# Layer norms applied in full with tokens on partitions, in a Mamba-2 and stick-breaking trunk on one core

## Chip, core and metric

The kernel runs on one core of a Trainium2 chip. The metric is the device time of one execution in microseconds (us). Runs of the same kernel differ by some tenths of a per cent: before the change the median of three runs is 1481.68 us (1478.76 to 1482.41).

## What is computed

Input and output are 512 tokens by 1024 channels in float32. The trunk has two layers. The first mixes tokens with a chunked state-space scan (SSD), the second with stick-breaking attention; an MLP with squared ReLU follows each. After each of the four sub-layers a layer norm is applied to the scaled residual plus the sub-layer's output:

```python
def layer_norm(x, g, b):
    mu = jnp.mean(x, axis=-1, keepdims=True)
    var = jnp.mean(jnp.square(x - mu), axis=-1, keepdims=True)
    return (x - mu) * lax.rsqrt(var + LN_EPS) * g + b

for layer in range(2):
    mix = mamba2_mixer(h, ...) if layer == 0 else stick_breaking_attention(h, ...)
    h = layer_norm(ALPHA * h + mix, ln_mix_g[layer], ln_mix_b[layer])
    h = layer_norm(ALPHA * h + squared_relu_mlp(h, ...), ln_mlp_g[layer], ln_mlp_b[layer])
```

So each norm's result has two uses: it is the input of the next sub-layer's matmuls, and it is the residual `h` that the sub-layer after it adds to.

## The kernel before

**Stages.** In order of time: the SSD mixer (to about 470 us), the first MLP (to about 820), attention (to about 1110), the second MLP (to the end). Every float32 matmul is made of three float32r matmuls (`mm3`, lines 159 to 162) on a rounded high part and a low part. So each operand is split: a copy to float32r gives the high part (`hh`, `wh`, `sp..h`, `w..h`), and a subtraction on VectorE (DVE) the low part (`hl`, `wl`, and so on). Weights come in tiles of 512 KB on SyncE's DMA queue in one fixed stream (`emit_w`): a transfer into a raw tile, a ScalarE copy (line 143) and a subtraction (line 145), mostly on DVE.

**Order.** The program is written for a tile framework that works out dependencies and semaphores. At build time it simulates the program and sets each engine's order of instructions from that; on the chip each engine works through its own list in that order. Within attention a hand-written filler spreads the projections of the next heads between the steps of 48 units (`z_stage`, `w_stage`, `pv_stage`).

**Output projections and norms.** `tok_out` computes a sub-layer's output with tokens on partitions. It adds it to the residual `v` (four token tiles of 128x1024) and takes statistics with `bn_stats`. In the last pass it works through the tokens in pairs of tiles (`PAIRS`), and for each pair calls the norm (`Norm.__call__`), and somewhat later its `turn`:

- `__call__` aggregates the statistics on DVE (line 284) and makes the inverse standard deviation with two small GpSimd steps (lines 286 and 287). For the first three norms one DVE `tensor_scalar` for each tile of 1024 columns then subtracts the mean and scales (line 300). The last norm, which has no successor, applies weight and bias too, from rows that are broadcast to all partitions: in two halves of 512 columns, two DVE instructions each (lines 293 and 295).
- `turn` transposes the pair in chunks on TensorE into PSUM (line 319). Channels now lie on partitions, so the norm's weight and bias are one number for each partition, and two ScalarE activations of 128x256 apply them on the way to a tile `hf` (line 322). DVE makes the high part with a cast (line 326) and the low part with a subtraction (line 327).

`v` itself then holds the normalised rows without weight and bias, and needs them before it can serve as the residual. `residual` does this on GpSimd: a multiplication and an addition for each 128x512 piece (lines 334 and 335), 16 instructions for each of the three norms. In the MLPs the 16 are emitted in one go after the first four output tiles (line 371). In attention one pair of them is emitted with every second unit (line 964). The rows for it are loaded on ScalarE's DMA queue by `load_rows` into one of the five large activation buffers.

**Covering work.** When the second pair of tokens is being normalised, TensorE already works on the first pair's columns of the next stage: in an MLP `proj` is called for 256 columns at a time over four output tiles (lines 366 to 368), in attention for the first key, query and value tiles (lines 932 to 936).

Of the kernel before, what the change touches and what calls it, by code (L numbers as in the profile page):

```python
# [11 lines left out]
F32 = mybir.dt.float32  # L12
# [5 lines left out]
P = 128  # L18
# [17 lines left out]
def trunk(ctx: ExitStack, tc: tile.TileContext, io):  # L36
# [46 lines left out]
    lnw = cp.tile([P, 4, 2, KD], F32, name="lnw")  # L83
# [175 lines left out]
    class Norm:  # L259
        def __init__(self, v, idx, name, final=False):  # L260
            self.v, self.idx, self.name, self.final = v, idx, name, final
            self.st = lp.tile([P, NT, 2, 6], F32, tag="st", name=f"{name}_st", bufs=2)
            self.mv = lp.tile([P, NT, 2], F32, tag="mv", name=f"{name}_mv", bufs=2)
            self.rs = lp.tile([P, NT], F32, tag="rs", name=f"{name}_rs", bufs=2)
            self.hl = None
            self.rows = None

            self.tmp = None

        def load_rows(self, pool):  # L270
            if pool is None:
                rows = act_tile(f"{self.name}_r").rearrange("p k t -> p (k t)")
                self.rows = [rows[:, j * D:(j + 1) * D] for j in range(2)]
            else:
                self.rows = [pool.tile([P, D], F32, tag=f"lnr{j}", name=f"{self.name}_r{j}", bufs=1)
                             for j in range(2)]
            for j in range(2):
                nc.scalar.dma_start(self.rows[j], io["lnrow"][self.idx, j].partition_broadcast(P))

        def __call__(self, grp):  # L280
            v, nm = self.v, self.name
            t0, t1 = grp[0], grp[-1] + 1
            for t in grp:
                nc.vector.bn_aggr(self.mv[:, t, :], self.st[:, t, :, :].rearrange("p m s -> p (m s)"))  # L284
            rs = self.rs[:, t0:t1]
            nc.gpsimd.tensor_scalar(rs, self.mv[:, t0:t1, 1], LN_EPS, None, ALU.add)  # L286
            nc.gpsimd.tensor_tensor(rs, rs, mhalf.to_broadcast([P, t1 - t0]), op=ALU.pow)
            if self.final:
                for t in grp:
                    for n in range(2):  # L290
                        c = slice(n * T, (n + 1) * T)
                        vs = v[:, t, c]
                        nc.vector.scalar_tensor_tensor(vs, vs, self.mv[:, t, 0:1], self.rows[0][:, c],
                                                       ALU.subtract, ALU.mult)
                        nc.vector.scalar_tensor_tensor(vs, vs, self.rs[:, t:t + 1], self.rows[1][:, c],
                                                       ALU.mult, ALU.add)
                        nc.sync.dma_start(io["out"][t * P:(t + 1) * P, c], vs)
                return
            for t in grp:
                nc.vector.tensor_scalar(v[:, t, :], v[:, t, :], self.mv[:, t, 0:1], self.rs[:, t:t + 1],  # L300
                                        ALU.subtract, ALU.mult)

        def turn(self, grp):
# [8 lines left out]
            for mm in range(KD // 2):  # L312
                pt = psum("bg", [P, 2, w], f"{nm}_b{mm}{t0}")
                hf = self.tmp[0].tile([P, T], F32, tag=self.tmp[1], name=f"{nm}_f{mm}{t0}", bufs=2)
                hf = hf.rearrange("p (j w) -> p j w", j=2)
# [4 lines left out]
                for j in range(2):  # L320
                    m = 2 * mm + j
                    nc.scalar.activation(hf[:, j, :], pt[:, j, :], AF.Identity,
                                         bias=lnw[:, self.idx, 1, m:m + 1], scale=lnw[:, self.idx, 0, m:m + 1])
                ms = slice(2 * mm, 2 * mm + 2)
                cs = slice(t0 * P, t1 * P)
                nc.vector.tensor_copy(hh[:, ms, cs], hf)  # L326
                nc.vector.tensor_sub(hl[:, ms, cs], hf, f(hh[:, ms, cs]))  # L327

        def residual(self):
            for t in range(NT):  # L330
                for n in range(2):
                    c = slice(n * T, (n + 1) * T)
                    vs = self.v[:, t, c]
                    tc.keep_in_program_order(nc.gpsimd.tensor_mul(vs, vs, self.rows[0][:, c]))
                    nc.gpsimd.tensor_add(vs, vs, self.rows[1][:, c])
                    yield
# [3 lines left out]
    def mlp(layer, ln, nxt):  # L340
        v, (hh, hl) = ln.v, ln.hl
        with tc.tile_pool(name=f"mlp{layer}", bufs=2, reuse_waits="tile") as mp:
            nxt.tmp = (mp, "r")
            ln.load_rows(None)
            for half in range(2):
# [16 lines left out]
                if half == 0:  # L362
# [8 lines left out]
                    for _ in ln.residual():  # L371
                        pass
# [11 lines left out]
                if half == 1 and nxt.final:  # L384
                    nxt.load_rows(mp)
# [5 lines left out]
    def ssm(sp, nxt_ln):  # L391
        nxt_ln.tmp = (sp, "sz")
# [29 lines left out]
        nc.scalar.dma_start(lnw, io["ln"])  # L422
# [290 lines left out]
        for g in range(G):  # L713
# [58 lines left out]
    def attention(ln, nxt):  # L772
# [4 lines left out]
        with tc.tile_pool(name="att", bufs=2, reuse_waits="tile") as at:  # L777
            nxt.tmp = (at, "wl")
            ln.load_rows(None)
# [163 lines left out]
            res = ln.residual()  # L943
            for s in range(len(units) + 3):
# [18 lines left out]
                if s >= 4 and s % 2 == 0:  # L963
                    next(res, None)
# [26 lines left out]
def layout(a):  # L991
# [25 lines left out]
    ln = np.stack([np.stack([a[f"ln_{n}_{s}"][l].reshape(KD, P).T for s in "gb"])  # L1017
                   for l in range(2) for n in ("mix", "mlp")])
    r["ln"] = ln.transpose(2, 0, 1, 3)
# [16 lines left out]
```

## Time and profile before

| | us |
|---|---|
| median of three runs | 1481.68 |
| lowest and highest | 1478.76 and 1482.41 |
| profiled execution | 1479.37 |
| its span, first to last instruction | 1477.6 |
| mean granted TensorE clock in the span | 0.994 |

In the rows, PE is TensorE's matmul work, PEld its weight loads, DVE VectorE, ACT ScalarE, POOL GpSimd and SP SyncE; a letter q behind the name is the engine's instruction queue. A row of a timeline begins with the start in us from the span's start and the duration in us; it names the engine, the line of the kernel, the operation, output<-input, the shapes and the count of instructions merged in it. A bracket at the end tells how long the engine had been idle before, and whose result ended that. Matmuls overlap in the pipeline, so a PE row's duration is longer than the distance to the next one.

### The profile page before, as it was taken

The page shows a single profiled execution, that of the slowest core. Times are in us where ns is not written, and L with a number is a line of the kernel's source. Part 1 is how long each engine was busy: PE and PEld are TensorE (multiplying, and loading weights), DVE is VectorE, ACT ScalarE, POOL GpSimd, SP SyncE. Part 2 cuts the span into 40 slices and gives each one's busy share as a digit, 9 for nine tenths or more (in the row PEclk, how much of TensorE's full clock was granted, in tenths as well). Part 3 has the DMA queues.
Part 4 walks back from the last instruction along what each step waited for, and adds up shares of the span by engine and source line. Part 5 has one row for each costly group of instructions (what it writes and reads, how often), then busy time and mean ns, then how long its engine had stood idle before and what let it go on. Part 6 is the DMA issues. An engine that isn't in the chain of part 4 may idle for free.

```text
span 1477.6 us, 19247 instructions
## 1 busy us (share of the span) xinstructions
PE 1445.0 (98%) x7606; PEld 1239.2 (84%) x7606; DVE 913.7 (62%) x1330; ACT 642.2 (43%) x1032; POOL 293.9 (20%) x291
## 2 busy tenths in 40 slices
PE   9999999999999999999999999999898999999997
PEld 7898897888988888888888997979688888888886
DVE  5799896568876862334423599998849533244334
ACT  5566663356652542123311476767524531133210
POOL 2345453235541610000000123100007000000001
PEclk9999999999999999999999999999999999999999
DMA  5232222322214343333321231111025433233311
GB/s 179 74 113 100 72 61 69 100 72 72 72 43 155 102 128 89 97 100 100 97 90 56 88 99 43 58 57 58 15 60 168 129 100 92 94 100 100 100 43 57
DMA packets 36763, 129.48 MB, mean 88 GB/s; under 512 B 4544, under 2 KB 4800, under 8 KB 36672
## 3 DMA queue, kind: packets, MB, share of 16 engines
q1 hardware_dynamic: 34800, 123.88, 26.6%
q10 hardware_dynamic: 1872, 4.37, 0.9%
q8 instruction: 60, 0.98, 0.3%
q14 instruction: 31, 0.25, 0.1%
HBM read 126.13 MB, written 2.10 MB: 87 GB/s over the span
## 4 chain that ended last, share of the span: by engine, by line
PE 81%; DVE 13%; ACT 2%; issue 2%; DMA 1%; POOL 0%; POOLq 0%; DVEq 0%; SPq 0%; ACTq 0%
PE f L161 16%; PE f L160 16%; PE f L162 16%; PE pz L160 2%; PE pz L162 2%; PE pz L161 2%; PE px L160 2%; PE px L162 2%; PE px L161 2%; DVE wl L145 1%; PE so L162 1%; PE so L160 1%; PE so L161 1%; PE pC L162 1%; PE pC L161 1%
## 5 line engine op out<-in xcount | busy, mean ns | idle before, releaser
L145 DVE TENSOR_TENSOR wl<-wr,wh 128x1024 fp32r<-128x1024 f32 x205 | 260.7, 1273 | 421.6 <-ACT wh L143 420.6
L143 ACT CAST wh<-wr 128x1024 fp32r<-128x1024 f32 x222 | 233.2, 1051 | 528.4 <-PE f L162 251.1
L161 PE MATMUL f<-ln_hl,wh 128*128 128x512 f32 (+1 forms) x576 | 210.0, 367 | 3.4 <-DVE ln_hl L327 3.4
L162 PE MATMUL f<-ln_hh,wl 128*128 128x512 f32 (+1 forms) x576 | 209.6, 366 | 0.0
L160 PE MATMUL f<-ln_hh,wh 128*128 128x512 f32 (+1 forms) x576 | 207.6, 367 | 1.1 <-DVE ln_hh L326 1.1
L286 POOL TENSOR_SCALAR ln_rs<-ln_mv 128x2 f32<-128x2 f32 (+1 forms) x10 | 5.2, 519 | 697.7 <-DVE ln_mv L284 697.7
L161 PEld LDWEIGHTS f<-ln_hl,wh 128*128 128x128 f32 x576 | 108.5, 189 | 21.5 <-DVE ln_hl L327 4.2
L162 PEld LDWEIGHTS f<-ln_hh,wl 128*128 128x128 f32 x576 | 108.6, 189 | 17.6
L160 PEld LDWEIGHTS f<-ln_hh,wh 128*128 128x128 f32 x576 | 107.2, 189 | 19.2 <-DVE ln_hh L326 1.5
L162 PE MATMUL pz<-wh,x_l 128*128 128x256 f32 x256 | 72.7, 284 | 0.0
L161 PE MATMUL pz<-wl,x_h 128*128 128x256 f32 x256 | 72.6, 284 | 0.0
L160 PE MATMUL pz<-wh,x_h 128*128 128x256 f32 x256 | 72.4, 283 | 0.0
L145 POOL TENSOR_TENSOR wl<-wr,wh 128x1024 fp32r<-128x1024 f32 x17 | 43.1, 2536 | 95.1 <-ACT wh L143 78.3
L160 PE MATMUL px<-x_h,wh 128*128 128x512 f32 x128 | 50.8, 397 | 0.0
L162 PE MATMUL px<-x_h,wl 128*128 128x512 f32 x128 | 50.3, 393 | 0.0
L161 PE MATMUL px<-x_l,wh 128*128 128x512 f32 x128 | 50.3, 393 | 0.0
L161 PEld LDWEIGHTS pz<-wl,x_h 128*128 128x128 f32 x256 | 48.8, 190 | 0.8
L160 PEld LDWEIGHTS pz<-wh,x_h 128*128 128x128 f32 x256 | 48.7, 190 | 0.8
L162 PEld LDWEIGHTS pz<-wh,x_l 128*128 128x128 f32 x256 | 48.8, 190 | 0.3
L350 ACT ACTIVATE r<-f 128x512 f32<-128x512 f32 x64 | 37.9, 592 | 20.7 <-DVE hd000l L359 16.3
L856 POOL TENSOR_TENSOR u<-u 128x128 f32<-128x128 f32 x16 | 9.3, 582 | 183.5 <-DVE u L854 183.5
L851 ACT ACTIVATE u<-z 128x384 f32<-128x384 f32 (+1 forms) x48 | 25.0, 524 | 39.4 <-DVE sp200l L860 7.0
(1348 smaller groups left out, 3918.0 us busy)
## 6 DMA issues: line engine op xcount, KB each, us to landing
wr<-w SPq DMA_DIRECT2D x128, 512.0 KB, 3.5
wr<-w_bc SPq DMA_DIRECT2D x16, 512.0 KB, 3.5
wr<-w_x SPq DMA_DIRECT2D x16, 512.0 KB, 3.5
wr<-w_z SPq DMA_DIRECT2D x16, 512.0 KB, 3.5
wr<-w_so SPq DMA_DIRECT2D x16, 512.0 KB, 3.5
wr<-w_qk SPq DMA_DIRECT2D x16, 512.0 KB, 3.6
ln_r<-lnrow ACTq DMA_DIRECT2D x8, 512.0 KB, 5.1
wr<-w_v SPq DMA_DIRECT2D x8, 512.0 KB, 3.6
```

Source lines behind the costliest of these rows:

```text
L143: nc.scalar.copy(hi, raw)
L145: eng.tensor_sub(lo, raw, f(hi))
L160: nc.tensor.matmul(out, a[0], b[0], start=start, stop=False, skip_group_check=skip)
L161: nc.tensor.matmul(out, a[0], b[1], start=False, stop=False, skip_group_check=skip)
L162: nc.tensor.matmul(out, a[1], b[0], start=False, stop=stop, skip_group_check=skip)
L286: nc.gpsimd.tensor_scalar(rs, self.mv[:, t0:t1, 1], LN_EPS, None, ALU.add)
L350: nc.scalar.activation(r, pt, AF.Relu)
L851: nc.scalar.activation(e, z, AF.Abs)
L856: nc.gpsimd.tensor_add(e4[:, n:], e[:, P:2 * P], e[:, 2 * P:])
```

## The change

Weight and bias are applied while tokens lie on partitions, in all four norms. The one `tensor_scalar` becomes two `scalar_tensor_tensor` instructions on DVE: `shift`, (v - mean) * weight row, and `scale`, (v * inverse deviation) + bias row. `turn` then only splits: a ScalarE copy out of PSUM makes the high part, and DVE subtracts it from PSUM for the low part. The residual pass, its rows in an activation buffer, the small table `lnw` and its load are dropped. The rows are loaded ahead of the norm: for the first in 512-column pieces into four buffers of the scan's decay matrices, for the second in whole rows into tiles of their own, for the third in 512-column pieces into the attention's work buffers behind the last unit, and for the last in 512-column pieces.

```diff
-        def load_rows(self, pool):
-            ...
+        def load_rows(self, make, width=D):
+            self.rows = []
+            for c0 in range(0, D, width):
+                seg = [c0, c0 + width]
+                for j in range(2):
+                    r = make(j, c0)
+                    nc.scalar.dma_start(r, io["lnrow"][self.idx, j, c0:c0 + width].partition_broadcast(P))
+                    seg.append(r)
+                self.rows.append(seg)
 ...
+            def shift(t, c0, c1, w):
+                vs = v[:, t, c0:c1]
+                nc.vector.scalar_tensor_tensor(vs, vs, self.mv[:, t, 0:1], w, ALU.subtract, ALU.mult)
+
+            def scale(t, c0, c1, b):
+                vs = v[:, t, c0:c1]
+                nc.vector.scalar_tensor_tensor(vs, vs, self.rs[:, t:t + 1], b, ALU.mult, ALU.add)
+                if self.final:
+                    nc.sync.dma_start(io["out"][t * P:(t + 1) * P, c0:c1], vs)
 ...
             for t in grp:
-                nc.vector.tensor_scalar(v[:, t, :], v[:, t, :], self.mv[:, t, 0:1], self.rs[:, t:t + 1],
-                                        ALU.subtract, ALU.mult)
+                for c0, c1, w, b in self.rows:
+                    shift(t, c0, c1, w)
+            for t in grp:
+                for c0, c1, w, b in self.rows:
+                    scale(t, c0, c1, b)
 ...
-                for j in range(2):
-                    m = 2 * mm + j
-                    nc.scalar.activation(hf[:, j, :], pt[:, j, :], AF.Identity,
-                                         bias=lnw[:, self.idx, 1, m:m + 1], scale=lnw[:, self.idx, 0, m:m + 1])
 ...
-                nc.vector.tensor_copy(hh[:, ms, cs], hf)
-                nc.vector.tensor_sub(hl[:, ms, cs], hf, f(hh[:, ms, cs]))
-
-        def residual(self):
-            ...
+                nc.scalar.copy(hh[:, ms, cs], pt)
+                nc.vector.tensor_sub(hl[:, ms, cs], pt, f(hh[:, ms, cs]))
 ...
     def mlp(layer, ln, nxt):
-            ln.load_rows(None)
 ...
-                    for _ in ln.residual():
-                        pass
 ...
-                if half == 1 and nxt.final:
-                    nxt.load_rows(mp)
+                if half == 1:
+                    nxt.load_rows(lambda j, c0: mp.tile([P, T if nxt.final else D], F32,
+                                                        tag=f"lnr{j}{c0 if nxt.final else 0}",
+                                                        name=f"lnr{layer}{j}{c0}", bufs=1),
+                                  T if nxt.final else D)
 ...
     def ssm(sp, nxt_ln):
-        nc.scalar.dma_start(lnw, io["ln"])
 ...
+                else:
+                    nxt_ln.load_rows(lambda j, c0: sp.tile(S4, F32, tag="dec", name=f"lnr{j}{c0}", bufs=4)
+                                     .rearrange("p a c -> p (a c)"), T)
 ...
     def attention(ln, nxt):
-            ln.load_rows(None)
-            res = ln.residual()
 ...
-                if s >= 4 and s % 2 == 0:
-                    next(res, None)
+            nxt.load_rows(lambda j, c0: at.tile([P, T], F32, tag=("u", "wf")[j], name=f"lnr{j}{c0}", bufs=2), T)
```

## Rows read from the trace of the kernel before

**Rows 1.** The page's first part: busy time, share of the span and instructions of each engine.
```profile
PE 1445.0 (98%) x7606; PEld 1239.2 (84%) x7606; DVE 913.7 (62%) x1330; ACT 642.2 (43%) x1032; POOL 293.9 (20%) x291
```

**Rows 2.** Busy time by stretches of the span. Columns: stretch and its length, busy us and count for PE, PEld, DVE, ACT and POOL, granted TensorE clock, share of DMA engines, GB/s. The first two stretches lie after the first norm, the next two round the third norm, the last is the tail of attention.
```profile
480.00:500.00 20.00, 20.00 (x149) 19.04 (x148) 12.70 (x14) 10.93 (x17) 7.35 (x4) 1.00 0.35 114
500.00:520.00 20.00, 20.00 (x90) 16.57 (x89) 19.93 (x12) 9.90 (x15) 19.53 (x13) 1.00 0.26 80
...
1100.00:1120.00 20.00, 18.84 (x119) 16.55 (x118) 15.24 (x23) 7.98 (x12) 4.94 (x6) 1.00 0.58 180
1120.00:1140.00 20.00, 16.63 (x131) 15.53 (x130) 19.39 (x13) 9.06 (x15) 19.53 (x13) 1.00 0.32 108
...
1040.00:1068.00 28.00, 22.87 (x101) 17.25 (x102) 23.84 (x47) 17.31 (x35) 1.22 (x2) 0.88 0.06 20
```

**Rows 3.** PE's timeline in attention, the rows with an idle time before them.
```profile
917.49 0.50 PE L903 MATMUL o<-w112l,vp 128*128 128x512 f32 x1 [0.67 <-DVE w112l L891]
...
918.90 0.33 PE L883 MATMUL z<-sp200h,none_r 128*128 128x128 f32 x1 [0.80 <-DVE sp200h L859]
...
920.59 0.33 PE L883 MATMUL z<-sp200l,none_r 128*128 128x128 f32 x1 [0.85 <-DVE sp200l L860]
...
978.09 0.44 PE L841 MATMUL z<-q,k 128*128 128x384 f32 x1 [0.88 <-ACT wf L887]
...
979.34 0.46 PE L903 MATMUL o<-w400h,vp 128*128 128x256 f32 x1 [0.57 <-DVE w400h L890]
...
990.68 0.39 PE L841 MATMUL z<-q,k 128*128 128x256 f32 x1 [0.44 <-ACT wf L887]
...
992.43 0.50 PE L903 MATMUL o<-w402h,vp 128*128 128x512 f32 x1 [0.32 <-DVE w402h L890]
```

**Rows 4.** Busy time by stretches, as in rows 2, for the two stretches of attention at a lower granted clock.
```profile
921.47:924.88 3.41, 3.41 (x17) 3.41 (x16) 2.59 (x3) 3.36 (x7) 0.00 (x0) 0.50 0.12 17
979.50:982.91 3.41, 3.41 (x9) 2.76 (x10) 3.28 (x7) 2.02 (x4) 0.00 (x0) 0.50 0.19 78
```

**Rows 5.** DVE's timeline in attention before and during the first gaps of rows 3.
```profile
913.47 0.42 DVE L890 CAST w112h<-wf 128x512 fp32r<-128x512 f32 x1
...
915.76 1.67 DVE L891 TENSOR_TENSOR w112l<-wf,w112h 128x512 fp32r<-128x512 f32 x1
917.36 1.49 DVE L859 CAST sp200h<-u 128x512 fp32r<-128x512 f32 x1
...
919.35 1.19 DVE L860 TENSOR_TENSOR sp200l<-u,sp200h 128x512 fp32r<-128x512 f32 x1
```

**Rows 6.** POOL's timeline at that time: the first and the last of four residual instructions in a row.
```profile
914.17 1.28 POOL L334 TENSOR_TENSOR v<-v,ln_r 128x512 f32<-128x512 f32 x1
...
918.64 1.35 POOL L335 TENSOR_TENSOR v<-v,ln_r 128x512 f32<-128x512 f32 x1
```

**Rows 7.** Groups of DVE instructions by line and shape from 480 to 500 us (after the first norm's second pair). Columns: count, busy us, mean ns of one, idle us before them and what ended it.
```profile
L327 DVE TENSOR_TENSOR ln_hl<-ln_f,ln_hh 128x512 fp32r<-128x512 f32 x4 | 2.8, 692 | 0.1
...
L326 DVE CAST ln_hh<-ln_f 128x512 fp32r<-128x512 f32 x4 | 1.7, 424 | 4.5 <-ACT ln_f L322 4.4
```

**Rows 8.** The same groups from 1120 to 1137 us (after the third norm's second pair).
```profile
L327 DVE TENSOR_TENSOR ln_hl<-ln_f,ln_hh 128x512 fp32r<-128x512 f32 x5 | 8.4, 1678 | 0.1
L326 DVE CAST ln_hh<-ln_f 128x512 fp32r<-128x512 f32 x4 | 5.5, 1367 | 0.5 <-ACT ln_f L322 0.5
```

**Rows 9.** PE's timeline at the start of the second MLP.
```profile
1113.28 0.38 PE L161 MATMUL f<-ln_hl,wh 128*128 128x256 f32 x1 [1.16 <-DVE ln_hl L327]
```

**Rows 10.** DVE's timeline: the first norm of the second pair, a weight subtraction, and one token tile of the last norm.
```profile
476.16 1.53 DVE L300 TENSOR_SCALAR v<-v,ln_mv,ln_rs 128x1024 f32<-128x1024 f32 x2 [0.92 <-POOL ln_rs L287]
...
1103.17 1.22 DVE L145 TENSOR_TENSOR wl<-wr,wh 128x1024 fp32r<-128x1024 f32 x1
...
1456.38 1.41 DVE L295 SCALAR_TENSOR_TENSOR v<-v,ln_rs,ln_r 128x512 f32<-128x512 f32 x2 [0.47 <-POOL ln_rs L287]
```

**Rows 11.** POOL's timeline: the two small steps of a norm, in the second norm and in the last.
```profile
811.99 0.22 POOL L286 TENSOR_SCALAR ln_rs<-ln_mv 128x2 f32<-128x2 f32 x1 [288.74 <-DVE ln_mv L284]
812.29 0.71 POOL L287 TENSOR_TENSOR ln_rs<-ln_rs,mhalf 128x2 f32<-128x2 f32 x1
...
1465.43 0.78 POOL L286 TENSOR_SCALAR ln_rs<-ln_mv 128x1 f32<-128x1 f32 x1 [3.64 <-DVE ln_mv L284]
1466.30 0.92 POOL L287 TENSOR_TENSOR ln_rs<-ln_rs,mhalf 128x1 f32<-128x1 f32 x1
```

**Rows 12.** PE's timeline at the start of the first MLP: two of its first matmuls and the transposes of the second pair.
```profile
470.07 0.28 PE L162 MATMUL f<-ln_hh,wl 128*128 128x256 f32 x1
470.19 0.28 PE L160 MATMUL f<-ln_hh,wh 128*128 128x256 f32 x1
...
479.79 0.60 PE L319 MATMUL ln_b<-ident,v 128*128 128x128 f32 x4
```

**Rows 13.** One line's instructions: a ScalarE copy of a 128x512 tile out of PSUM. Columns: count, shortest, median and longest ns, first and last start.
```profile
L615 ACT COPY cbm<-cb x8: 573/586/597, 65.0 to 417.6; 128x512 f32<-128x512 f32 x8
```

**Rows 14.** The loads of the norms' rows: the issuing instruction, with columns as in rows 13.
```profile
L278 ACTq DMA_DIRECT2D ln_r<-lnrow x8: 334/392/688, 469.7 to 1129.3; - x8
...
DMA to landing us min/median/max: 4.0/5.1/6.2
```

**Rows 15.** PE's timeline at the end of the SSD stage.
```profile
445.76 0.51 PE L160 MATMUL so<-wx,yT4h 128*128 128x512 f32 x1 [1.20 <-DVE v L248]
```

More of the change, by code (lines that the diff above doesn't have):

```diff
@@ L82, in trunk @@
     nw = cp.tile([P, 16], F32, name="nw")
-    lnw = cp.tile([P, 4, 2, KD], F32, name="lnw")
     stream = []
@@ L266, in __init__ @@
             self.rows = None
-            self.tmp = None
-        def load_rows(self, pool):
[L271 to L276, printed above, removed]
-            for j in range(2):
-                nc.scalar.dma_start(self.rows[j], io["lnrow"][self.idx, j].partition_broadcast(P))
+        def load_rows(self, make, width=D):
[7 more added lines that the diff above has]
+                self.rows.append(seg)
         def __call__(self, grp):
@@ L287, in __call__ @@
             nc.gpsimd.tensor_tensor(rs, rs, mhalf.to_broadcast([P, t1 - t0]), op=ALU.pow)
+            def shift(t, c0, c1, w):
[6 more added lines that the diff above has]
+                    nc.sync.dma_start(io["out"][t * P:(t + 1) * P, c0:c1], vs)
             if self.final:
                 for t in grp:
[L290 to L293, printed above, removed]
-                                                       ALU.subtract, ALU.mult)
-                        nc.vector.scalar_tensor_tensor(vs, vs, self.rs[:, t:t + 1], self.rows[1][:, c],
-                                                       ALU.mult, ALU.add)
-                        nc.sync.dma_start(io["out"][t * P:(t + 1) * P, c], vs)
+                    for c0, c1, w, b in self.rows:
+                        shift(t, c0, c1, w)
+                        scale(t, c0, c1, b)
                 return
             for t in grp:
-                nc.vector.tensor_scalar(v[:, t, :], v[:, t, :], self.mv[:, t, 0:1], self.rs[:, t:t + 1],
-                                        ALU.subtract, ALU.mult)
+                for c0, c1, w, b in self.rows:
+                    shift(t, c0, c1, w)
+            for t in grp:
+                for c0, c1, w, b in self.rows:
+                    scale(t, c0, c1, b)
         def turn(self, grp):
@@ L319, in turn @@
                         nc.tensor.transpose(pt[:, j, (t - t0) * P:(t - t0 + 1) * P], v[:, t, m * P:(m + 1) * P], ident)
-                for j in range(2):
-                    m = 2 * mm + j
-                    nc.scalar.activation(hf[:, j, :], pt[:, j, :], AF.Identity,
-                                         bias=lnw[:, self.idx, 1, m:m + 1], scale=lnw[:, self.idx, 0, m:m + 1])
                 ms = slice(2 * mm, 2 * mm + 2)
                 cs = slice(t0 * P, t1 * P)
-                nc.vector.tensor_copy(hh[:, ms, cs], hf)
-                nc.vector.tensor_sub(hl[:, ms, cs], hf, f(hh[:, ms, cs]))
-        def residual(self):
[L330 to L336, printed above, removed]
+                nc.scalar.copy(hh[:, ms, cs], pt)
+                nc.vector.tensor_sub(hl[:, ms, cs], pt, f(hh[:, ms, cs]))
     PAIRS = [(0, 1), (2, 3)]
@@ L391, in ssm @@
     def ssm(sp, nxt_ln):
-        nxt_ln.tmp = (sp, "sz")
         x_h, x_l = act_pair("x_")
@@ L1016, in layout @@
     r["x"] = a["x"][0]
-    ln = np.stack([np.stack([a[f"ln_{n}_{s}"][l].reshape(KD, P).T for s in "gb"])
-                   for l in range(2) for n in ("mix", "mlp")])
-    r["ln"] = ln.transpose(2, 0, 1, 3)
     r["lnrow"] = np.stack([np.stack([a[f"ln_{n}_{s}"][l] for s in "gb"]) for l in range(2) for n in ("mix", "mlp")])
```

4 lines of the change are left out of this document (removed).

## The prediction

> **What bounds the kernel now.** I read the page's busy times first. TensorE (PE) is busy 1445.0 us, 98% of the span [rows 1], and the change alters no matmul and no transpose, so its time can only come from the few places where PE waits or runs at a lower clock. Next I cut the span into stretches [rows 2]. After the first norm PE is busy 20.00 of 20 us, and it stays so in the next stretch, although GpSimd runs the residual pass there and keeps VectorE (DVE) at 19.93. Round the third norm PE is busy 18.84 and then 16.63. So the same pass costs nothing in the first MLP and may cost 3.4 us in the second.
>
> The attention stage is the other place. In its tail PE is busy 22.87 of 28 us [rows 2], but the residual pass is over by then. Earlier, its PE timeline [rows 3] has gaps of 0.67, 0.80 and 0.85 us between 916.8 and 920.6 us (2.32 in sum), each ended by a DVE result, and 2.21 us in four gaps between 977 and 993 us. Each group is followed by 3.41 us in which the granted clock was 0.50 against 1.00, that is 1.2 GHz instead of 2.4 [rows 4]. At half clock PE does 1.7 us of work in those 3.41, so 1.7 us is lost each time.
>
> Then I asked who held DVE up. Just before the first group of gaps a 128x512 two-input subtraction took 1.67 us, a cast 1.49 and another subtraction 1.19 [rows 5], while GpSimd ran four residual instructions back to back [rows 6]. The same cast takes 0.42 a little earlier [rows 5], and the same kind of subtraction 0.69 after the first norm [rows 7]. The excess is 0.98 + 1.07 + 0.50 = 2.55 us: nearly the 2.32 that PE lost. After the third norm the casts average 1.37 and the subtractions 1.68 us [rows 8], against 0.42 and 0.69 for the same lines after the first [rows 7].
>
> That reading has a rule beside it. The Trainium skill (SBUF — State Buffer, section "Who interferes with whom") says that VectorE and GpSimd share one port pair as an exclusive lock, which a cast in a two-port mode, or an instruction with two SBUF inputs against a GpSimd one that reads SBUF, must wait for. The 1.67 against 0.69 us agrees.
>
> **The change, part by part.**
>
> *Residual pass removed in the second MLP.* The five gaps that make the 3.37 us of the 1120 to 1140 stretch [rows 2] end on the slowed casts and subtractions [rows 8]. With no pass beside them they should run as after the first norm, where the same loops left PE no gap [rows 2, 7]: **-3.4**. Bounds 0 (another wait comes next) and -3.4.
>
> *Residual pass removed in attention.* The gaps of 2.32 us go with the excess of 2.55, and with them the half-clock stretch that followed: -2.32 - 1.7 = **-4.0**. Bounds 0 and -4.0. What is late next there is the chain through ScalarE that the later gaps show. The gaps of 977 to 993 [rows 3] come some 57 us later, and two of the four end on a ScalarE exponential rather than on DVE. They can be lag carried over from the slowed part, or DVE's own load. I take half of 2.21 + 1.7: **-2.0**, with bounds 0 and -3.9.
>
> *Norm in two passes.* Before, two tokens' rows were normalised by two one-source instructions, 1.53 us together, after GpSimd's two steps. Now each token tile of 1024 columns takes a shift and a scale, both with two tensor inputs. The last norm has them already: two of 512 columns take 1.41 us [rows 10]. So a pair of tiles costs 8 x 0.70 = 5.6 us of DVE against 1.53 (with 1024 columns in one instruction somewhat less). The shift doesn't need GpSimd's result, so GpSimd's 0.22 and 0.71 us [rows 11] pass beside it: the chain from statistics to the last scale grows from about 1.0 + 1.5 to 5.6, by 3.1 us. Against this stand the four casts of the first pair, now gone from DVE: 4 x 0.42 = 1.7 us [rows 7]. So the second pair's norm ends some 1.4 us later.
>
> What covers this at the first norm: by 470.1 PE is at the first half of the tokens, with 96 matmuls 0.12 us apart, 11.5 us in all [rows 12], and the transposes of the second pair stand at 479.79, while the norm before ended at 476.16 + 1.53 = 477.7 [rows 10, 12]. That is 2.1 us of slack against 1.4. The second norm is built alike. I take **0** for both; if the cover is gone (one weight subtraction of 1.2 us more in front [rows 10]) up to 1.5 us each, so 0 to +3.
>
> A row that speaks against this part: in the last norm GpSimd's two steps took 0.78 and 0.92 us beside the shifts, against 0.22 and 0.71 alone [rows 11]. Even so the 1.7 us pass beside 2.8 us of shifts, and the sum is unchanged. By the rule of that section of the Trainium skill each step may wait for one whole shift, so the 1024-column shifts of the second norm would give 2 x 1.4 + 0.9 = 3.7 us, +0.9 on the chain there.
>
> *After the transposes.* Each chunk of 128x512 had two ScalarE instructions, a DVE cast and a DVE subtraction. Now ScalarE copies once (0.59 us for that shape out of PSUM [rows 13]) and DVE subtracts once, about 0.69. This is shorter by the cast, 0.42 us for each chunk; where PE has no gap it gives nothing: 0. But a PSUM buffer is now held until DVE has read it. That matters at the third norm alone, where the projection's second column half sits in the same four buffers. There PE already waited 1.16 us for the first subtraction [rows 9]. Two opposite effects, the cast gone and the buffer late: **+0.5**, with bounds -1.2 (gap gone) and +2.7 (plus one half-clock loss and a us of its own).
>
> *Rows and the small load.* Three norms now load their two rows early on ScalarE's queue, in the third behind the last attention unit. An issue took 0.39 us in the middle [rows 14], so four cost 1.6 us of that queue. At the end of the SSD stage PE waits anyway (1.20 us at 445.76 [rows 15]) in a chain of weight transfer, copy and subtraction; if the rows' 1 MB stands before a weight tile, a row transfer of 512 KB takes 5 us to land [rows 14]. I take **+0.5**, with bounds 0 and +3. The loads that go (the same rows, later, and the small table) hid under full PE stretches: 0.
>
> Sum: -3.4 - 4.0 - 2.0 + 0.5 + 0.5 = **-8.4 us**. The profiled execution took 1479.37 us, so it would take 1471.0; the median of the three runs is 1481.68, 2.3 above it, and the forecast in those terms is 1473.3 us.
>
> **Rivals.**
>
> *The attention stalls are not GpSimd's.* PE also lost time at 977 to 993 [rows 3], and DVE is nearly full there by its own load, 3.28 of 3.41 us [rows 4]; the lost 2.3 us may come back a few units later. Against it: the excess equals the gaps. Then only the second MLP gains: -3.4 + 1.0 = -2.4, 1479.3 us.
>
> *Full return.* The relieved DVE also clears the later gaps: -3.4 - 1.2 - 4.0 - 3.9 = -12.5, 1469.2 us; clearing some of the 5.1 us that PE lacks in the tail of attention [rows 2] could add 3. For it: that same DVE load. Against it: nothing in the rows ties the stall at 978 us to a GpSimd instruction.
>
> *Slower: PE runs dry at the norms.* The longer DVE chain of the second pair, with weight subtractions queued between, ends after the 11.5 us of covering matmuls are spent. It decides once the chain is later by some 3 to 4 us instead of 1.4. A dry spell of 2 us is what cost a half-clock stretch in attention [rows 3, 4], so each of three norms would lose 2.0 + 1.7, 11 us; with attention's gain undone as well, -3.4 + 11 = +7.6, 1489.3 us. Against it: PE's order fills from 96 independent matmuls.
>
> **How the numbers follow.** Forecast 0.50, full return 0.15, stalls not GpSimd's 0.24, PE dry 0.11. About 0.3% (4.4 us) can be told from no change. The first two lie beyond it: faster 0.65; the third within: 0.24; the last: 0.11. The range reaches from the full return with part of the tail, 1466, over the third case to 1484, with the positive bounds of the norm and row terms; it leaves out most of the dry case.
>
> **What would show it.** Right: no GpSimd instruction over 1 us after 460 us but weight subtractions; casts near 0.42 and subtractions near 0.69 in attention and at the start of the second MLP; PE 20 of 20 us after the third norm; one half-clock stretch fewer in attention. Wrong: PE gaps ended by a shift, a scale or a transpose at any norm; the same gaps in attention with casts at 0.42; a longer PE wait at the end of the SSD stage ended by a transfer.

## The result, and the profile after

| | before | after |
|---|---|---|
| median of 4 runs each, us (lowest to highest) | 1481.95 (1478.76 to 1482.41) | 1466.99 (1466.41 to 1467.21) |
| ratio of times, 95% interval | | 0.9907 (0.9893 to 0.9921) |
| profiled execution, us (span) | 1479.37 (1477.6) | 1466.94 (1464.9) |

The change saves 12.4 us between the two profiled executions and 15.0 between the medians. That is faster, by 0.9% and well beyond the 0.3% that can be told from no change; the forecast was 1473.3 us, within 1466 to 1484. The direction held, and the gain is larger than the forecast 8.4: half as large again between the profiled executions, 1.8 times by the medians.

The page's first part of the changed kernel answers to [rows 1]:

```profile
PE 1439.3 (98%) x7606; PEld 1237.5 (84%) x7606; DVE 880.4 (60%) x1334; ACT 632.2 (43%) x1008; POOL 222.9 (15%) x243
```

GpSimd lost 71 us of work, VectorE 33 and ScalarE 10. The number of matmuls is the same. So what counts is where TensorE waited or ran slowly. Next come stretches of the changed kernel with the columns of [rows 2] and [rows 4]. The first three lie after the first and third norm, the next four cut the span from the second norm to the start of the second MLP into stages, and the last two are the parts of attention at the lower clock.

```profile
480.00:500.00 20.00, 20.00 (x148) 18.93 (x147) 13.92 (x18) 12.54 (x18) 2.44 (x1) 1.00 0.55 183
500.00:520.00 20.00, 20.00 (x90) 16.56 (x89) 9.12 (x12) 8.72 (x12) 0.00 (x0) 1.00 0.37 110
1114.00:1134.00 20.00, 20.00 (x152) 19.21 (x152) 14.37 (x20) 12.54 (x18) 0.00 (x0) 1.00 0.48 154
...
820.00:850.00 30.00, 30.00 (x240) 29.17 (x239) 20.85 (x30) 11.51 (x19) 4.75 (x9) 1.00 0.26 83
850.00:1000.00 150.00, 147.96 (x888) 132.77 (x887) 130.22 (x237) 107.10 (x200) 6.78 (x11) 1.00 0.20 65
1000.00:1096.00 96.00, 90.73 (x455) 76.49 (x454) 70.25 (x130) 47.81 (x87) 4.62 (x7) 0.95 0.16 50
1096.00:1150.00 54.00, 53.76 (x343) 48.55 (x342) 38.47 (x54) 24.29 (x34) 2.49 (x3) 1.00 0.50 160
...
1040.87:1044.28 3.41, 3.41 (x14) 2.92 (x15) 2.38 (x6) 2.25 (x6) 0.00 (x0) 0.50 0.00 0
1051.11:1057.94 6.83, 6.71 (x20) 5.25 (x20) 6.42 (x14) 3.13 (x6) 0.00 (x0) 0.50 0.11 40
```

PE's idle time is a stretch's length less its busy time. From 850 to 1000 us it is 2.04 (4.76 in the same stretch before), from 1096 to 1150 it is 0.24 (4.54 before), and after the first norm 0.00, as it was. Of the half-clock stretches the two of [rows 4] have gone. In the tail of attention the clock is low for 3.41 + 6.83 us, against a single 6.83 (from 1058 us) before.

PE's timeline after, at the places of [rows 15] and [rows 3]; these are its only rows with 0.3 us or more of idle time from 440 to 470 us and from 850 to 1000 us:

```profile
445.70 0.50 PE L159 MATMUL so<-wx,yT4h 128*128 128x512 f32 x1 [1.32 <-DVE v L247]
...
973.20 0.44 PE L829 MATMUL z<-q,k 128*128 128x384 f32 x1 [1.93 <-ACT wf L875]
```

The gaps of 916.8 to 920.6 us are gone, and so is the 1.16 of [rows 9]. The four later gaps of attention have shrunk to one of 1.93, nearly their sum of 2.21.

Where the time went is read best by following the same matmul through both PE timelines (start in us):

| the first matmul that reads | before | after | difference |
|---|---|---|---|
| sp111l with ntri_ge (second head pair) | 903.52 | 903.53 | 0.0 |
| w212l | 949.56 | 943.90 | -5.7 |
| w502l | 1017.45 | 1009.34 | -8.1 |
| sp710l with ntri_ge (last pair) | 1059.83 | 1053.02 | -6.8 |
| ln_hh and wh, second MLP | 1111.21 | 1103.61 | -7.6 |
| (end of the span) | 1477.6 | 1464.9 | -12.7 |

Nothing was gained or lost in the first 903 us. Attention gives 7.6 us, three quarters of it between 903 and 950, and the second MLP gives 5.1. Four transposes of the third norm, 0.4 us of work, stand ahead of the last mark before and behind it after; counted alike, attention gives 7.2 and the second MLP 5.5.

### The profile page after: what moved, and what is told of

It is laid out like the page before. It is cut to its first block, busy times and chain, and to the rows that moved or that the text cites. A ratio compares the mean times of both kernels' runs of the same rounds, so it can differ in the third digit from the quotient of the medians.

```text
span 1464.9 us, 19160 instructions
## 1 busy us (share of the span) xinstructions
PE 1439.3 (98%) x7606; PEld 1237.5 (84%) x7606; DVE 880.4 (60%) x1334; ACT 632.2 (43%) x1008; POOL 222.9 (15%) x243
## 4 chain that ended last, share of the span: by engine, by line
PE 88%; DVE 7%; ACT 2%; DMA 1%; issue 1%; POOL 0%; POOLq 0%; DVEq 0%; SPq 0%; ACTq 0%
PE f L160 16%; PE f L159 16%; PE f L161 16%; PE pz L159 2%; PE pz L161 2%; PE pz L160 2%; PE px L159 2%; PE px L161 2%; PE px L160 2%; PE z L873 1%; PE so L161 1%; PE so L159 1%; PE so L160 1%; PE o L891 1%; PE pv L159 1%
## 5 line engine op out<-in xcount | busy, mean ns | idle before, releaser
L144 DVE TENSOR_TENSOR wl<-wr,wh 128x1024 fp32r<-128x1024 f32 x205 | 252.8, 1234 | 443.8 <-ACT wh L142 443.3
L283 POOL TENSOR_SCALAR ln_rs<-ln_mv 128x2 f32<-128x2 f32 (+1 forms) x10 | 8.9, 887 | 745.8 <-DVE ln_mv L281 745.8
L339 ACT ACTIVATE r<-r 128x512 f32<-128x512 f32 x64 | 40.6, 634 | 2.1
```

The source lines that it names most:

```text
L144: eng.tensor_sub(lo, raw, f(hi))
L339: nc.scalar.activation(r, r, AF.Square)
```

## The experiments

Each is compared with runs of the kernel before on its own chip (medians 1479.44 to 1481.29 us). "The pass" is what GpSimd did for the residual. In kernels built from the changed one it is replayed as two multiplications by one for each 128x512 piece of v, in the same places.

**The kernel before without its pass** (norms and transposes as before; the weight and bias rows and GpSimd's two instructions per piece are out, so the residual lacks them).

```diff
-            ln.load_rows(None)
...
-                    for _ in ln.residual():
-                        pass
...
-            ln.load_rows(None)
...
-            res = ln.residual()
...
-                if s >= 4 and s % 2 == 0:
-                    next(res, None)
```

> The kernel before with the residual pass and the loads of its rows taken out (the residual then lacks the norms' weight and bias; the inputs of the matmuls keep them). Pass theory (GpSimd's pass holds VectorE up in attention and at the start of the second MLP): 1467 to 1471 us, most of the measured gain of 15, with the 1.16 us wait at the third norm left. Split theory (the gain is the shorter way after the transposes): no change, 1480 to 1482. Order theory (the gain comes from another order drawn up at build time): anywhere, with no fewer slowed casts to go with it.

Measured 1469.74 us, ratio 0.9938 (0.9926 to 0.995): dropping the pass alone gives 9.8 us against before's 1479.58, where the changed kernel's repeat, further down, gives 12.6. The start of the second MLP, by stretches:

```profile
1096.00:1150.00 54.00, 52.83 (x339) 47.73 (x338) 35.73 (x54) 26.25 (x40) 2.35 (x4) 1.00 0.43 147
```

The one PE row with over 0.3 us of idle time at the third norm:

```profile
1112.78 0.38 PE L161 MATMUL f<-ln_hl,wh 128*128 128x256 f32 x1 [1.17 <-DVE ln_hl L327]
```

The idle time at the start of the second MLP falls from 4.54 to 1.17 us, by the 3.37 that the prediction put on the pass. What is left is the gap of [rows 9], unmoved. So the pass didn't cause that gap, and the change removes it by its other part. In time the pass cost more than that idle time: from the first matmul of the second MLP (1110.70) to the end of the span (1472.3) this run takes 361.6 us, and before took 366.4. In attention it takes 40.6 us from the sp111l to the w212l of the table above (905.94 to 946.52), against 46.0 before and 40.4 after. Its profiled execution is the slowest of the five (1474.29): it is already 2.6 us late at the first matmul of the first MLP (472.35 against 469.72), so stretches can be compared and starts can't.

**The changed kernel with the pass back in attention alone.**

```diff
+    ones4 = one.unsqueeze(1).to_broadcast([P, 4, P])
...
+    def passes(v, pool):
+        for t in range(NT):
+            for n in range(2):
+                vs = v[:, t, n * T:(n + 1) * T].rearrange("p (a c) -> p a c", a=4)
+                tc.keep_in_program_order(nc.gpsimd.tensor_mul(vs, vs, ones4))
+                nc.gpsimd.tensor_mul(vs, vs, ones4)
+                yield
...
+            res = passes(v, at)
...
+                if s >= 4 and s % 2 == 0:
+                    next(res, None)
```

> The kernel after with 16 GpSimd multiplications of the residual by one (128x512 each, two after every second attention unit, where the pass was). Pass theory: attention is 8 us longer again, 1474 to 1476 us, with gaps on PE ended by casts of 1.4 to 1.5 us. Split theory and order theory: 1466 to 1468.

Measured 1475.18 us, ratio 0.997 (0.9959 to 0.9981): 8.2 us slower than the changed kernel. DVE's timeline at the gaps of [rows 3]:

```profile
916.39 0.93 DVE L857 CAST sp200h<-u 128x512 fp32r<-128x512 f32 x1
917.25 1.43 DVE L857 CAST sp201h<-u 128x384 fp32r<-128x384 f32 x1
918.59 1.75 DVE L858 TENSOR_TENSOR sp200l<-u,sp200h 128x512 fp32r<-128x512 f32 x1
```

POOL's timeline there, the first and the last of four pass instructions in a row, as in [rows 6]:

```profile
914.31 1.29 POOL L334 TENSOR_TENSOR v<-v,ones_r 128x512 f32<-128x512 f32 x1
...
918.54 1.26 POOL L335 TENSOR_TENSOR v<-v,ones_r 128x512 f32<-128x512 f32 x1
```

The PE row with the largest idle time in that place:

```profile
920.40 0.41 PE L881 MATMUL z<-sp200l,none_r 128*128 128x128 f32 x1 [2.29 <-DVE sp200l L858]
```

And the stretch that follows, with the columns of [rows 4]:

```profile
920.50:923.91 3.41, 3.41 (x15) 3.41 (x16) 2.17 (x3) 3.36 (x6) 0.00 (x0) 0.50 0.00 0
```

Four GpSimd instructions in a row, a slowed cast and subtraction, a PE gap of 2.29 (2.32 in three gaps before) and 3.41 us at half clock come back at the same place. The matmuls of the table above then start at 903.77, 949.45, 1017.76 and 1060.34, within 0.5 us of before, and the second MLP's first at 1110.35, 0.9 earlier than before. So at least 6.7 of attention's 7.6 us are the pass's. Each edit also draws up another order of instructions at build time, and that alone could move the time. But the run before this one had the old code without the pass and lost the stalls, and this one has the new code with it and gets them back, with the slowed instructions beside GpSimd's.

**The pass back in the second MLP alone.**

```diff
+                    if layer == 1:
+                        for _ in passes(v, mp):
+                            pass
                     extra[:] = [mp, 2, 2, False, marks[1 + 2 * layer]]
```

(`passes` as in the run before.)

> The kernel after with the same 16 GpSimd multiplications by one at the start of the second MLP, where the pass was. Pass theory as predicted: +4 to +5 us, 1471 to 1472. Pass theory with the port rule taken strictly: VectorE's one instruction for each chunk now reads PSUM and one SBUF tile, which need not wait for GpSimd, so +0 to +1.5 us, 1467 to 1468.5, the scales and weight subtractions alone being slowed. Split theory: no change.

Measured 1469.37 us, ratio 0.9921 (0.991 to 0.9933), 2.4 above the changed kernel by medians: more than the strict rule gave, less than the prediction did. Its DVE groups from 1108 to 1125 us, with columns as in [rows 7]:

```profile
L291 DVE SCALAR_TENSOR_TENSOR v<-v,ln_rs,lnr 128x512 f32<-128x512 f32 x4 | 6.8, 1770 | 0.6 <-POOL ln_rs L284 0.6
L144 DVE TENSOR_TENSOR wl<-wr,wh 128x1024 fp32r<-128x1024 f32 x3 | 6.3, 2137 | 0.4 <-ACT wh L142 0.4
L326 DVE TENSOR_TENSOR ln_hl<-ln_b,ln_hh 128x512 fp32r<-128x512 f32 x4 | 2.6, 681 | 0.1
```

PE's rows with an idle time from 1090 to 1130 us:

```profile
1114.68 0.87 PE L322 MATMUL ln_b<-ident,v 128*128 128x128 f32 x6 [0.52 <-DVE v L291]
1116.36 0.87 PE L322 MATMUL ln_b<-ident,v 128*128 128x128 f32 x6 [0.81 <-DVE v L291]
```

Beside the same GpSimd work the new subtraction, which reads one operand from PSUM, keeps 0.68 us. The scale and the weight subtraction, with two SBUF operands, take 1.77 (0.75 alone) and 2.14 (1.22 alone). The idle time from 1096 to 1150 us is 1.38 against 0.24 us, +1.1. The rest of the 2.4 isn't in this profile, whose execution was the fastest of the five, 1465.15 at a mean clock of 0.997; three others took 1469.4 to 1469.8 at 0.994.

**Before's transposes and split put back** (ScalarE copies out of PSUM in two instructions, DVE casts and subtracts from SBUF), in three forms: with nothing else, with the pass in the second MLP, and with GpSimd there only writing memory.

```diff
-                nc.scalar.copy(hh[:, ms, cs], pt)
-                nc.vector.tensor_sub(hl[:, ms, cs], pt, f(hh[:, ms, cs]))
+                hf = self.tmp[0].tile([P, T], F32, tag=self.tmp[1], name=f"{nm}_f{mm}{t0}", bufs=2)
+                hf = hf.rearrange("p (j w) -> p j w", j=2)
+                for j in range(2):
+                    nc.scalar.activation(hf[:, j, :], pt[:, j, :], AF.Identity)
+                nc.vector.tensor_copy(hh[:, ms, cs], hf)
+                nc.vector.tensor_sub(hl[:, ms, cs], hf, f(hh[:, ms, cs]))
...
```

The third has, in place of the pass's two multiplications:

```diff
+        scr = pool.tile([P, 3 * T], F32, name="scr", bufs=1)
...
-                tc.keep_in_program_order(nc.gpsimd.tensor_mul(vs, vs, ones4))
-                nc.gpsimd.tensor_mul(vs, vs, ones4)
+                tc.keep_in_program_order(nc.gpsimd.memset(scr, 1.0))
+                nc.gpsimd.memset(scr, 2.0)
```

> The kernel after with the old split after the transposes (two ScalarE instructions into an SBUF tile, a cast and a subtraction), and no residual pass. Pass theory: only the wait at the third norm comes back, with one half-clock stretch at most, 1467 to 1471 us. Split theory (the shorter split is worth what the run with old split and pass lost): 1475 to 1482.

> As the run before, but with the old split after the transposes (two ScalarE instructions into an SBUF tile, then a cast and a subtraction that read SBUF). Port rule: casts near 1.4 and subtractions near 1.7 us again, PE gaps of 3 to 5 us after the third norm, 1470 to 1472.5 us. Split theory: the same time, but with casts at 0.42.

> The kernel after with the old split, and at the start of the second MLP 16 GpSimd memsets of 128x1536 (they write and read nothing) where the run with old split and pass had multiplications. Port rule: casts are slowed, subtractions of two SBUF tiles keep 0.69 us; 1470 to 1477 us. If any GpSimd work slows VectorE: as with the pass, 1480 to 1484. If only GpSimd's reads do: as the old split alone.

Measured 1473.61 (ratio 0.9956, 0.9944 to 0.9968), 1482.41 (1.0019, 1.001 to 1.0027) and 1472.68 (0.9954, 0.9942 to 0.9966). The first lies above what the pass theory allowed and below the other, so neither had it: the old split alone costs 6.6 us. Two PE rows of the kernel with the old split alone:

```profile
470.20 0.39 PE L160 MATMUL f<-ln_hl,wh 128*128 128x256 f32 x1 [0.33 <-DVE ln_hl L331]
...
827.21 0.38 PE L161 MATMUL pv<-wh,ln_hl 128*128 128x256 f32 x1 [0.80 <-DVE ln_hl L331]
```

PE now waits for the subtraction at the first norm, where neither kernel of the change does, and for 0.80 us at the second, where before waited 0.16 (at 826.49) and the changed kernel doesn't wait. The second head pair starts 2.8 us late (906.28). Whether this is the old split's doing or that of the long norm beside it is settled further down, with the one-pass norm. Of the rest, a half-clock stretch behind a gap of 1.93 us at 976 us (the repeat of the changed kernel has one too) takes 1.3 us up to w502l, and about 3 us fall between the last head pair and the second MLP, where no run here singles out a cause.

The second adds 8.8 us. The start of its second MLP, by stretches:

```profile
1096.00:1150.00 54.00, 47.39 (x291) 41.82 (x290) 50.39 (x59) 18.62 (x33) 29.27 (x20) 0.94 0.35 120
```

Its DVE groups from 1112 to 1138 us:

```profile
L331 DVE TENSOR_TENSOR ln_hl<-ln_f,ln_hh 128x512 fp32r<-128x512 f32 x7 | 9.7, 1391 | 0.1
L292 DVE SCALAR_TENSOR_TENSOR v<-v,ln_rs,lnr 128x512 f32<-128x512 f32 x4 | 6.8, 1765 | 0.0
L330 DVE CAST ln_hh<-ln_f 128x512 fp32r<-128x512 f32 x6 | 6.8, 1131 | 0.0
```

PE is idle 6.61 us there against 1.05 with the old split alone (+5.6), and a mean clock of 0.94 over 54 us, where it was 1.00, takes some 3.2 more. That adds up to the 8.8 between the medians, but in part by chance: in the two profiled executions the second MLP takes 371.3 us (from 1108.99) against 361.5 (from 1110.73), 9.8 more, since a gap costs more than its idle time. The expectation lacked both the old split's own price and this half clock.

The third runs 16 GpSimd memsets of 1.4 to 1.5 us through the same time. DVE groups from 1116 to 1130 us:

```profile
L330 DVE CAST ln_hh<-ln_f 128x512 fp32r<-128x512 f32 x5 | 5.4, 1087 | 1.1 <-ACT ln_f L329 1.1
L331 DVE TENSOR_TENSOR ln_hl<-ln_f,ln_hh 128x512 fp32r<-128x512 f32 x5 | 3.4, 689 | 0.1
L292 DVE SCALAR_TENSOR_TENSOR v<-v,ln_rs,lnr 128x512 f32<-128x512 f32 x4 | 2.7, 737 | 0.0
```

A GpSimd that only writes slows the casts (1.09 against 0.42 us) and leaves the instructions with two SBUF inputs alone (0.69, 0.74), and PE loses nothing: 0.87 us idle from 1096 to 1150. The Trainium skill (SBUF — State Buffer, section "Who interferes with whom") says just that: an instruction with two SBUF inputs contends with a GpSimd one that reads SBUF, not with one that only writes. These rows agree, and so does the 0.68 of the subtraction out of PSUM beside the reading pass.

**The changed kernel with a one-pass norm** (the first three norms leave out weight and bias).

```diff
-                for c0, c1, w, b in self.rows:
-                    shift(t, c0, c1, w)
...
+                nc.vector.tensor_scalar(v[:, t, :], v[:, t, :], self.mv[:, t, 0:1], self.rs[:, t:t + 1],
+                                        ALU.subtract, ALU.mult)
```

> The kernel after with one tensor_scalar for each tile in the first three norms in place of shift and scale (weight and bias of those norms are left out). If the longer VectorE chain is covered by PE's work on the first pair, as predicted: no change, 1465 to 1468 us. If the chain costs something that PE does not show: 2 us or more faster.

Measured 1469.08 us, ratio 0.9928 (0.9915 to 0.994): no faster than the two-pass norm (1466.99), and rather slower. Its idle time from 820 to 850 us (0.00) and from 1096 to 1150 (0.24) is that of the changed kernel; a gap of 0.92 us at 984.27 is new. Why the shorter norm is 2 us slower stays open beyond that gap.

With it, all four pairings of norm and split have been run. The time from the first matmul of the first MLP to the sp111l of the table above, which holds the first and the second norm, in us:

| | one-pass norm | two-pass norm |
|---|---|---|
| old split | 433.8 (before, 469.72 to 903.52); 433.6 (before without its pass, 472.35 to 905.94) | 436.9 (469.35 to 906.28) |
| short split | 433.8 (469.55 to 903.33) | 433.9 (the changed kernel, 469.66 to 903.53) |

Neither the old split nor the longer norm costs anything there by itself; together they cost 3.0 us. So in this stretch the short split pays for the long norm.

**The pass back in the first MLP alone** (as in the second, with `layer == 0`).

> The kernel after with 16 GpSimd multiplications of the residual by one at the start of the first MLP, where the pass was. Pass theory with PE's cover: casts and subtractions slowed there, no gap on PE, 1466 to 1468 us. If a slowed VectorE costs time wherever it is: 3 to 6 us more, 1470 to 1473.

Measured 1467.74 us, ratio 0.992 (0.9906 to 0.9935), the changed kernel's own time within 0.8:

```profile
500.00:520.00 20.00, 20.00 (x90) 16.57 (x89) 19.90 (x12) 8.59 (x12) 19.61 (x11) 1.00 0.32 106
```

DVE is full, GpSimd is full, and PE misses nothing: what the prediction read from the first MLP holds.

**The changed kernel again**, on another chip.

> The kernel after once more, beside the three that follow: 1464 to 1469 us by every theory.

Measured 1467.02 us (1466.45 to 1468.56), ratio 0.9915 (0.9902 to 0.9927). Its profiled execution was the slowest one, and shows by what. Its one PE row with an idle time from 960 to 1000 us:

```profile
973.51 0.44 PE L829 MATMUL z<-q,k 128*128 128x384 f32 x1 [1.93 <-ACT wf L875]
```

The stretch behind it:

```profile
974.32:977.73 3.41, 3.41 (x9) 2.83 (x10) 3.32 (x7) 2.07 (x4) 0.00 (x0) 0.50 0.14 58
```

The same kernel, the same gap of 1.93 us, and this time a half-clock stretch behind it. Its first matmul that reads w212l is 0.3 us later than in the other execution (944.21), and the one that reads w502l 1.8 (1011.12): the 1.5 in between are nearly all of the 1.6 us between 1468.56 and 1466.94.

**Is the gap at 973 us VectorE's load?** Three versions of the changed kernel: the 16 small additions of attention moved from GpSimd to VectorE; this, with the three later value projections put into other head pairs (1, 3, 5 in place of 0, 2, 5, counted from 0); and the same with 0, 3, 5.

```diff
-                    nc.gpsimd.tensor_add(e4[:, n:], e[:, P:2 * P], e[:, 2 * P:])
+                    nc.vector.tensor_add(e4[:, n:], e[:, P:2 * P], e[:, 2 * P:])
...
-    v_at = (0, 2, 5)
+    v_at = (1, 3, 5)
```

> The kernel after with attention's last regular GpSimd work, 16 additions of 128x128, moved to VectorE. Pass theory carried on: VectorE takes about 0.2 us for each, is no longer held up by GpSimd and waits for no GpSimd result there; 1464 to 1467 us. If VectorE's own load sets attention's later gaps: 1467 to 1470.

> As the run before, and the three later value projections, PE's work between the units, are put into the head pairs 1, 3 and 5 instead of 0, 2 and 5. If the gap of 1.9 us near 973 us is VectorE's own load in a stretch without that work: it goes, with the half-clock stretch that sometimes follows; 1461 to 1465 us. If it comes from the units' chain itself: as the run before.

> As the run with the additions on VectorE, with the value projections in the head pairs 0, 3 and 5. If the gaps sit where a stretch has no such work: neither those of 861 to 877 us (pair 0, seen with 1, 3 and 5) nor that of 973 us (pair 3, seen with 0, 2 and 5) comes, though the pairs 1 and 2 now follow each other without it; 1460 to 1464 us. If the gap only moves to pair 2, near 945 us: 1464 to 1467.

Measured 1465.6 (ratio 0.9907, 0.9892 to 0.9922), 1464.81 (0.99, 0.9884 to 0.9917) and 1466.28 (0.9899, 0.9882 to 0.9915). In the first, the gap stays, 1.69 us at 972.65, with 0.67 at 983.23. PE's rows with gaps in attention before 1000 us, for 1, 3, 5:

```profile
861.07 0.33 PE L871 MATMUL z<-sp000l,none_r 128*128 128x128 f32 x1 [0.38 <-DVE sp000l L848]
863.21 0.44 PE L829 MATMUL z<-q,k 128*128 128x384 f32 x1 [0.84 <-ACT wf L875]
876.40 0.50 PE L891 MATMUL o<-w002h,vp 128*128 128x512 f32 x1 [1.01 <-DVE w002h L878]
```

For 0, 3, 5:

```profile
919.78 0.44 PE L829 MATMUL z<-q,k 128*128 128x384 f32 x1 [2.74 <-ACT wf L875]
```

The gap moves to head pairs that run without a value projection beside them: the first pair (0) in one, the turn from pair 1 to pair 2 in the other, where of the two outcomes named ahead the second came: the gap only moved. So the gap that the prediction couldn't tie to GpSimd sits where PE lacks other work to fill in while the chain from scores to weights runs; it is there without the pass too. Lacking that work is not enough, though: with 1, 3, 5 the pairs 2 and 4 run without it as well, and have no gap. With 1, 3, 5 the kernel is the best of all, 2.2 us below the changed one by medians, though the intervals of the ratios overlap; 1.4 of the 2.2 came with the moved additions.

## Why the prediction was right, and where it was mis-sized

*Pass removed in the second MLP, -3.4*: the wait was right, its price too small. With the pass alone taken out, PE's idle time there fell by 3.37 us as said, but the time by 4.7 (366.4 to 361.6). The prediction priced a gap by its idle time, and a gap costs more. PE's timeline before at one of the five:

```profile
1127.74 0.28 PE L161 MATMUL f<-ln_hl,wh 128*128 128x256 f32 x1
1128.84 0.38 PE L161 MATMUL f<-ln_hl,wh 128*128 128x256 f32 x1 [0.82 <-DVE ln_hl L327]
1129.07 0.28 PE L162 MATMUL f<-ln_hh,wl 128*128 128x256 f32 x1
```

Matmuls of this shape start 0.12 us apart [rows 12]. Here two starts are 1.10 and 0.23 apart, 1.09 more than 2 x 0.12 for 0.82 of idle time: the restart costs 0.27 us. Five of them make 1.3, and 3.4 + 1.3 is the 4.7.

*Pass removed in attention, -4.0*: the mechanism was right, and the replay showed each link of it; the term was too small. The matmuls after the gaps start 5.7 us earlier. The prediction summed the gaps' idle time, 2.32, and 1.7 for the clock. Three restarts add 0.8. The other 0.9 us lie ahead of the gaps, as the same matmul before and after shows:

```profile
907.26 0.34 PE L883 MATMUL z<-sp111l,none_r 128*128 128x384 f32 x1
...
906.32 0.34 PE L871 MATMUL z<-sp111l,none_r 128*128 128x384 f32 x1
```

Before, PE waits 0.15 us at 904.71 and restarts there (some 0.7), and one matmul of 0.23 us more stands in between. With the pass put back there is a wait of 0.22 us again, at 905.68.

*Later gaps, -2.0*: 2.4 were gained by 1009 us, but not in the way described. The gaps didn't halve: one of 1.93 us stands for the four, and the kernel before without the pass has it too (1.92 us at 975.82). What went in this execution is their half-clock stretch, and the repeat shows that it can return. In the tail 1.3 us were given back, since 3.41 us more at half clock fell there; no term had this.

*Norm in two passes, 0*: the 0 held, but not by the sum that gave it. The second pair's last scale ends 2.5 us later than before (480.15 against 477.7), where 1.4 was forecast and 2.1 was the slack, and PE still has no gap: the second pair's transposes start at 480.80 in place of 479.79, behind more of the next stage's matmuls. The two parts of the 1.4 were off as well. The chain from the end of the last statistics (475.35, and 474.68 before) to the last scale grew by 1.8 us and not 3.1, since the first token's two shifts run ahead of those statistics; and the four casts that went did not bring the statistics forward, which came 0.7 later. DVE's timeline after, at the first and the second norm, answers to [rows 10]:

```profile
475.38 1.41 DVE L287 SCALAR_TENSOR_TENSOR v<-v,ln_mv,lnr 128x512 f32<-128x512 f32 x2
477.41 2.74 DVE L291 SCALAR_TENSOR_TENSOR v<-v,ln_rs,lnr 128x512 f32<-128x512 f32 x4 [0.61 <-POOL ln_rs L284]
...
828.41 1.28 DVE L287 SCALAR_TENSOR_TENSOR v<-v,ln_mv,lnr 128x1024 f32<-128x1024 f32 x1
830.61 2.49 DVE L291 SCALAR_TENSOR_TENSOR v<-v,ln_rs,lnr 128x1024 f32<-128x1024 f32 x2 [0.91 <-POOL ln_rs L284]
```

POOL's timeline at the same two norms answers to [rows 11]:

```profile
475.44 0.78 POOL L283 TENSOR_SCALAR ln_rs<-ln_mv 128x2 f32<-128x2 f32 x1 [13.38 <-DVE ln_mv L281]
476.30 1.07 POOL L284 TENSOR_TENSOR ln_rs<-ln_rs,mhalf 128x2 f32<-128x2 f32 x1
...
828.47 1.30 POOL L283 TENSOR_SCALAR ln_rs<-ln_mv 128x2 f32<-128x2 f32 x1 [13.20 <-DVE ln_mv L281]
829.85 0.72 POOL L284 TENSOR_TENSOR ln_rs<-ln_rs,mhalf 128x2 f32<-128x2 f32 x1
```

GpSimd's step of 0.22 us takes 1.30 beside a shift of 1.28, so the scales wait 0.61 and 0.91 us. The claim that the small steps pass beside the shifts was wrong by that much. At the second norm the second step took 0.72, about its 0.71 alone: DVE was idle by then (from 829.69 to 830.61). At the first norm it started beside the second of two shifts of 0.70 and took 1.07. The exclusive lock that the Trainium skill states in SBUF — State Buffer, section "Who interferes with whom", agrees with these rows: the steps that met a shift took longer, the one that met none did not.

*After the transposes, 0, and at the third norm +0.5*: this is the step that failed. The shorter split was costed at nothing because PE had no gap. But it is what covers the longer norm: with the old split beside the two-pass norm the first two norms take 3.0 us more, and the whole kernel 6.6. And at the third norm the late release of PSUM cost nothing, while the gap of [rows 9] went. DVE's groups after, from 1112 to 1129 us, answer to [rows 8]:

```profile
L291 DVE SCALAR_TENSOR_TENSOR v<-v,ln_rs,lnr 128x512 f32<-128x512 f32 x4 | 2.7, 748 | 0.6 <-POOL ln_rs L284 0.6
L326 DVE TENSOR_TENSOR ln_hl<-ln_b,ln_hh 128x512 fp32r<-128x512 f32 x4 | 2.5, 684 | 3.0 <-ACT ln_hh L325 3.0
```

DVE now waits 3.0 us for ScalarE's copies there, where it was the late one. Idle time fell from 4.54 us to 0.24, so this part brought about -0.9 (1.17 without the pass, less 0.24), near its bound of -1.2 and not the +0.5 taken. With the 4.7 of the pass that is the second MLP's 5.5 to within 0.1.

*Rows, +0.5*: about +0.1. The wait at the end of the SSD stage is 1.32 us against 1.20.

Of the signs named beforehand, casts and subtractions in attention came out as said. PE is busy 20 of 20 us after the third norm, as said. Groups of DVE from 855 to 950 us after:

```profile
L848 DVE TENSOR_TENSOR sp200l<-u,sp200h 128x512 fp32r<-128x512 f32 x1 | 0.7, 686 | 0.0
L847 DVE CAST sp100h<-u 128x512 fp32r<-128x512 f32 x1 | 0.4, 429 | 0.6 <-POOL u L844 0.6
```

"No GpSimd instruction over 1 us" did not hold, by the small steps above, and one half-clock stretch fewer in number, as said, hides that the tail's grew. Of the rivals, full return (1469.2 us) came nearest in time, and half of it in mechanism: the gap at the third norm went, the later gap of attention stayed. That the stalls weren't GpSimd's is refuted by the replay. PE did not run dry at a norm, but with the old split it began to.

Luck has a part in the size: the half-clock stretch at 979 us was missing in this execution of the changed kernel and is there in the repeat's. Open: why the one-pass kernel is 2 us slower; about 3 us of the old split's 6.6; and 1.3 of the 2.4 us that the pass in the second MLP adds by medians.

## What to carry to other kernels

When PE waits for VectorE, look at what GpSimd does in the same microseconds and where the slowed instructions have their operands: one with an operand in PSUM kept its time beside GpSimd's reads, one with both in SBUF took 1.8 to 2.4 times as long. Price a PE gap with its restart, 0.27 us here, and with the half-clock stretch that may follow. A shorter chain with no gap behind it isn't worthless: if the same change lengthens the work ahead of it, try the two apart before costing either at zero.

## What the runs showed of the hardware

- A 128x2 step on GpSimd took 1.30 us beside a VectorE instruction of 1.28 us with two SBUF operands, and 0.22 alone [rows 11].
- GpSimd memsets slowed VectorE's casts from 0.42 to 1.09 us and not its two-input instructions (0.69 and 0.74).
- A PE wait of 0.82 us delayed the matmuls behind it by 1.09 us.
- A PE gap of 1.93 us was followed by 3.41 us at 1.2 GHz in one execution and by none in another of the same kernel.
